# A hybrid decoder layer on one core: in the second feed-forward part, gate and up of ten chunks are computed as pairs with seven block products in two of four k steps

## The chip, the cores and the metric

The kernel runs on one core of one Trainium2 chip. The metric is the device time of one execution in microseconds. The engines are named as in the profile: PE (TensorE, matrix products), PEld (its weight loads), DVE (VectorE), ACT (ScalarE), POOL (GpSimd) and SP (SyncE, which issues most DMAs).

## What is computed

A decoder layer over 256 positions with a model width of 2048, in f32: a first SwiGLU feed-forward part (width 5632), a mixer (a state-space group beside a gated group, with a projection in and out), a second SwiGLU part, a gated per-layer embedding, and norms. The change is in the second feed-forward part:

```
def swiglu(x, w_gate, w_up, w_down):
    return (jax.nn.silu(x @ w_gate) * (x @ w_up)) @ w_down
h = h + 0.5 * swiglu(rms_norm(h, norm_ffn2[i]), w2_gate[i], w2_up[i], w2_down[i])
```

x is 256 by 2048, w_gate and w_up are 2048 by 5632, w_down is 5632 by 2048.

## The kernel before

**Products.** Every f32 product a·w is made of three matmuls of rounded parts: a high, w high; a high, w low; a low, w high. The activations (transposed, in hTh and hTl) are the stationary operand, 128 by 128; the weights stream as 512 columns. The weights come from DRAM as raw tiles of four k tiles by 512 columns (1 MB), and each half of a tile (two k tiles) is split: ACT copies it to `wh` in the rounded type (line 133), DVE subtracts to give `wl` (line 134). There are three raw buffers and four of each split (`LA_SPLIT` + 1).

**Order.** A program-wide list `plan` holds groups (one weight matrix, 512 columns) and their k steps. `stream` walks it in sub-steps of two k tiles: 12 matmuls for both blocks of 128 positions (t = 0, 1), into two accumulators. Before the products of sub-step i it emits the splits up to i + 3. A raw load is issued on SP two loads ahead; it waits for the last split that read its buffer. After a group's last sub-step its `post` is started; a post is a generator whose `yield n` puts its next piece n ticks later, and a tick is one sub-step. So a piece that is emitted after the products of sub-step i stands in the queues of DVE and ACT behind the split of i + 3 and ahead of that of i + 4. All engines work their queues in order.

**The feed-forward part** (`ffn_groups`, called for both). It takes 11 chunks of 512 columns. Per chunk there is a gate group (16 k tiles, 8 sub-steps) and an up group. `gate_post` puts silu of the scaled gate into g (ACT, line 393); `up_post` multiplies with up on DVE (line 404), and `flip` turns g: two 32x32 block transposes on DVE (line 367), a write to a DRAM scratch `gsc` (POOL queue, line 370) and four reads back (line 373). Six ticks later ACT and DVE split the turned g into gT (lines 203, 204). The down groups then run over 44 k tiles in the order of the chunks. gT is held in SBUF for all 11 chunks, in two tiles, gTa (six chunks) and gTb (five).

**PSUM.** Two pools of four banks: `acc` for the groups, `aux` for transposes and the mixer's small products. In the feed-forward part a chunk's gate and up take two `acc` banks each.

**Before the second part** the output projection of the mixer updates h (line 900), and `h_to_T` turns h into hTh and hTl: by `flip` and scaling for column blocks 0 and 2 in this place, by PE transposes for 1 and 3.

Of the kernel before, what the change touches and what calls it, by code (L numbers as in the profile page):

```python
# [15 lines left out]
P = 128  # L16
# [5 lines left out]
NW = 512  # L22
# [25 lines left out]

class Group:
    def __init__(self, w, n0, kt, act, post, kbase=0):  # L50
        self.w, self.n0, self.kt, self.act, self.post, self.kbase = w, n0, kt, act, post, kbase
        self.ps = None


class Layer:
# [38 lines left out]
    def stream(self):  # L94
        nc = self.nc
        subs, loads = [], []
        for g, k0, nk in self.plan:
            li = len(loads)
            loads.append((g, k0, nk))
# [3 lines left out]
        tail = self.plan[-1][0]  # L103
        n_tail = sum(sb[0] is tail for sb in subs)
        raws, split = {}, {}
# [10 lines left out]

        def do_split():
            i = state["sp"]
            state["sp"] += 1
            g, li, s0, k0, nk = subs[i]  # L120
            while state["ld"] <= min(li + 2, len(loads) - 1):
                load(state["ld"])
                state["ld"] += 1
            for f in self.presplit.pop(i, ()):
                f()
            src = raws[li][:, s0:s0 + nk, :]
# [11 lines left out]
        def products(i, ts, ps=None, c0=0, c1=NW):  # L138
            g, li, s0, k0, nk = subs[i]
            wh, wl = split[i]  # L140
            for j in range(nk):
                k = k0 + j
                for t in ts:
                    ah, al = g.act(k, t)
                    first, last = k == 0, k == g.kt - 1
                    o = (ps or g.ps[t])[:, c0:c1]
                    nc.tensor.matmul(o, ah, wh[:, j, c0:c1], start=first, stop=False)  # L147
                    nc.tensor.matmul(o, ah, wl[:, j, c0:c1], start=False, stop=False)  # L148
                    nc.tensor.matmul(o, al, wh[:, j, c0:c1], start=False, stop=last)  # L149

        for i in range(n):
            ahead = i + LA_SPLIT + 1
            if i > n - 2 * n_tail:
                ahead += (i - (n - 2 * n_tail)) // 2
            while state["sp"] < min(ahead, n):
                do_split()
            g, li, s0, k0, nk = subs[i]
            if k0 == 0:
                g.ps = [self.acc_p.tile([P, NW], F32, tag="acc", name=f"acc{t}") for t in range(2)]
            if g is tail:  # L160
                products(i, (0,))
            else:
                products(i, range(2))
                split.pop(i)
            if k0 + nk == g.kt:
                self.spawn(g.post(g, 0, 0) if g is tail else g.post(g))
            self.tick_no += 1
            self.run_due()
        late = self.acc_p.tile([P, NW], F32, tag="acc", name="late")
        for part, ps in enumerate((tail.ps[1], late)):  # L170
            for i in range(n - n_tail, n):
                products(i, (1,), ps, part * NW // 2, (part + 1) * NW // 2)
# [52 lines left out]
    def h_to_T(self, n, gcol, flip):  # L225

        if flip:
# [9 lines left out]
            for t in range(2):  # L237
                self.nc.vector.tensor_tensor(out=dl[:, t], in0=trv[:, t], in1=dh[:, t].bitcast(F32), op=ALU.subtract)
            return
        for b in range(2):  # L240
# [4 lines left out]
            self.split_gain2(ps, self.gcol[:, gcol + k0:gcol + k0 + 2], self.hTh[:, k0:k0 + 2], self.hTl[:, k0:k0 + 2])  # L245

# [3 lines left out]
    def kernel(self):  # L250
# [23 lines left out]
        self.gsc = [dram.tile([P, 4 * 256], F32, name=f"gsc{b}") for b in range(2)]  # L274
        self.spot = 0
# [13 lines left out]
        self.open("gta", "gt")  # L289
        self.open_g()  # L290
# [40 lines left out]
    def open(self, key, name, bufs=1):  # L331
        p = self.tc.tile_pool(name=name, bufs=bufs)
        self.pools[key] = p.__enter__()
        self.cms[key] = p
# [6 lines left out]
    KA = 24  # L341

    def open_g(self):
        n = self.KA // 4
        self.gT_a = (self.pools["gta"].tile([P, n, 4 * 256], F32R, name="gTah"),
                     self.pools["gta"].tile([P, n, 4 * 256], F32R, name="gTal"))
        self.open("gs", "gs")

    def open_gb(self):
        self.open("gtb", "gtb")  # L350
        n = 11 - self.KA // 4
        self.gT_b = (self.pools["gtb"].tile([P, n, 4 * 256], F32R, name="gTbh"),
                     self.pools["gtb"].tile([P, n, 4 * 256], F32R, name="gTbl"))

    def gT_at(self, c):
        if c < self.KA // 4:
            return self.gT_a, c
        return self.gT_b, c - self.KA // 4

    def flip(self, src):  # L360
# [9 lines left out]
        nc.gpsimd.dma_start(out=sc, in_=tr)  # L370
        sv = sc.rearrange("(i f) (a x) -> a f i x", i=4, a=4)
        for a in range(4):
            nc.gpsimd.dma_start(out=tr[32 * a:32 * a + 32, :].rearrange("f (i x) -> f i x", i=4), in_=sv[a])  # L373
        return tr

    def ffn_groups(self, which):
# [5 lines left out]
        def gate_post(c):  # L382
            def post(g):
                if which == 2 and c == 0:
                    self.close_mix()
                    self.open("gta", "gt")
                    self.open_g()
                    self.open_gb()
# [8 lines left out]
        def up_post(c):  # L397
            def post(g):
                gt = st.pop(c)
                if which == 1 and c == 6:  # L400
                    self.close("wrk")
                    self.open_gb()
# [3 lines left out]
                (th, tl), k = self.gT_at(c)  # L406
                tr = self.flip(gt)
                yield 6
                self.split_plain(tr.rearrange("p (i b u) -> p b i u", i=4, b=8),
                                 th[:, k, :].rearrange("p (b i u) -> p b i u", b=8, i=4),  # L410
                                 tl[:, k, :].rearrange("p (b i u) -> p b i u", b=8, i=4))
            return post

        def act_g(k, t):
            x, c = self.gT_at(k // 4)
# [17 lines left out]
        for c in range(11):  # L433
            gate = Group(wg, c * NW, 16, self.act_hT, gate_post(c))
            if which == 1 and c == 0:
                self.plan += [(gate, 0, 1), (gate, 1, 1)] + [(gate, k, 2) for k in (2, 4, 6)] + [(gate, 8, 4), (gate, 12, 4)]
            else:
                self.whole(gate)
            self.whole(Group(wu, c * NW, 16, self.act_hT, up_post(c)))
        for n in range(4):  # L440
            self.whole(Group(wd, n * NW, 44, act_g, down_post(n)))
# [216 lines left out]
    def close_mix(self):  # L658
        for n in ("yss", "mix", "qt"):
            self.close(n)  # L660

    def open_mix(self):
        for n in ("gtb", "gs", "gta"):
            self.close(n)
        self.open("qt", "qt", 2)
# [296 lines left out]
    def ple_groups(self):  # L962
# [4 lines left out]
        def prep():  # L967
            for n in ("gtb", "gs", "gta"):
# [161 lines left out]
```

## Time and profile before

| | before |
|---|---|
| median of 3 runs | 1851.09 us (1850.9 to 1851.18) |
| the profiled execution's own time | 1851.49 us |
| its span, first to last instruction | 1849.8 us |
| PE busy | 1837.9 us (99%), 8512 matmuls |
| DVE busy | 1140.3 us (62%), 1541 instructions |
| ACT busy | 854.5 us (46%) |
| POOL busy | 131.0 us (7%) |
| DMA | 405.10 MB, mean 219 GB/s |
| mean granted TensorE clock | 0.998 |

Times on the timeline are microseconds from the span's start. A PE that is busy is not a PE at its peak: matmuls are pipelined, so a recorded matmul lasts longer than the distance to the next one. The second feed-forward part begins at about 1022 us with the first gate, its down product at about 1501 us.

### The profile page before, as it was taken

To read this page: it belongs to the slowest core of one execution; us is meant where nothing else is said; L and a number is where in the kernel's file an instruction comes from. 1 tells how busy PE (TensorE), PEld (TensorE's weight loads), DVE (VectorE), ACT (ScalarE), POOL (GpSimd) and SP (SyncE) were. 2 spreads that over 40 slices of the span, in tenths; PEclk is the share of its full clock that TensorE was granted. 3 is DMA by queue.
4 is the path that set the end of the run, shared out by engine and by line. 5 is a ranking of instruction groups with operands and counts; after the bars stand their busy time and mean duration, and the time that the engine had idled before them with its cause. 6 is when DMAs were issued, how large, how long until landed. Compare 5 with 4: busy or idle time off the path is not lost.

```text
span 1849.8 us, 21900 instructions
## 1 busy us (share of the span) xinstructions
PE 1837.9 (99%) x8512; PEld 1526.8 (83%) x8512; DVE 1140.3 (62%) x1541; ACT 854.5 (46%) x1012; POOL 131.0 (7%) x208
## 2 busy tenths in 40 slices
PE   9999999999999999999999999999999999999998
PEld 7888888888888888888888888888888888888887
DVE  6788886555545554698876555555555555455565
ACT  6444444444444444444446544444444444444454
POOL 1000000000000000022100000000000000000000
PEclk9999999999999999999999999999999999999999
DMA  8677777666656665665546666666666665566553
GB/s 324 223 244 265 235 269 253 217 217 226 220 201 216 216 216 193 225 253 210 188 163 216 213 216 217 217 226 219 222 218 217 216 216 206 204 216 216 190 204 134
DMA packets 72615, 405.10 MB, mean 219 GB/s; under 512 B 10176, under 2 KB 15552, under 8 KB 29888
## 3 DMA queue, kind: packets, MB, share of 16 engines
q1 hardware_dynamic: 62000, 371.67, 56.4%
q0 software_dynamic: 10080, 31.47, 5.8%
q8 instruction: 66, 1.08, 0.2%
q10 hardware_dynamic: 432, 0.57, 0.1%
q14 instruction: 37, 0.30, 0.0%
HBM read 376.28 MB, written 27.26 MB: 218 GB/s over the span
## 4 chain that ended last, share of the span: by engine, by line
PE 98%; DMA 1%; issue 1%; DVE 0%; ACT 0%; SPq 0%; POOLq 0%; POOL 0%; DVEq 0%; ACTq 0%
PE acc L147 32%; PE acc L149 32%; PE acc L148 32%; PE tr L199 1%; PE y L759 1%; DMA raw<-in_w_gate 1%; PE v L712 0%; PE sp L800 0%; PE mps L623 0%; PE y L753 0%; DVE wl L134 0%; ACT wh L133 0%; SPq L296 0%; DVE hg L1052 0%; DVE h L1035 0%
## 5 line engine op out<-in xcount | busy, mean ns | idle before, releaser
L134 DVE TENSOR_TENSOR wl<-raw,wh 128x1024 fp32r<-128x1024 f32 (+1 forms) x649 | 800.9, 1237 | 642.5 <-ACT wh L133 640.7
L133 ACT ACTIVATE wh<-raw 128x1024 fp32r<-128x1024 f32 (+1 forms) x649 | 685.9, 1059 | 824.3 <-PE acc L149 779.6
L147 PE MATMUL acc<-wh,hTh 128*128 128x512 f32 (+1 forms) x1744 | 680.9, 390 | 0.1
L148 PE MATMUL acc<-wl,hTh 128*128 128x512 f32 (+1 forms) x1744 | 678.1, 389 | 1.3 <-DVE wl L134 1.3
L149 PE MATMUL acc<-wh,hTl 128*128 128x512 f32 (+1 forms) x1744 | 678.2, 389 | 0.0
L148 PEld LDWEIGHTS acc<-wl,hTh 128*128 128x128 f32 x1744 | 327.5, 188 | 69.1 <-DVE wl L134 2.1
L149 PEld LDWEIGHTS acc<-wh,hTl 128*128 128x128 f32 x1744 | 327.4, 188 | 68.2
L147 PEld LDWEIGHTS acc<-wh,hTh 128*128 128x128 f32 x1744 | 327.4, 188 | 67.8 <-ACT wh L133 0.5
L147 PE MATMUL acc<-wh,gTah 128*128 128x512 f32 x384 | 149.4, 389 | 0.0
L148 PE MATMUL acc<-wl,gTah 128*128 128x512 f32 x384 | 149.4, 389 | 0.0
L149 PE MATMUL acc<-wh,gTal 128*128 128x512 f32 x384 | 149.4, 389 | 0.0
L147 PE MATMUL acc<-wh,gTbh 128*128 128x512 f32 x320 | 124.5, 389 | 0.0
L148 PE MATMUL acc<-wl,gTbh 128*128 128x512 f32 x320 | 124.5, 389 | 0.0
L149 PE MATMUL acc<-wh,gTbl 128*128 128x512 f32 x320 | 124.5, 389 | 0.0
L370 POOL DMA_DIRECT2D gsc<-tr x30 | 17.0, 568 | 1160.1 <-DVE tr L367 1160.1
L147 PEld LDWEIGHTS acc<-wh,gTah 128*128 128x128 f32 x384 | 72.1, 188 | 15.1
L148 PEld LDWEIGHTS acc<-wl,gTah 128*128 128x128 f32 x384 | 72.1, 188 | 15.0
L149 PEld LDWEIGHTS acc<-wh,gTal 128*128 128x128 f32 x384 | 72.1, 188 | 14.9
L373 POOL DMA_DIRECT2D tr<-gsc x120 | 65.5, 552 | 97.4 <-DMA gsc<-tr 91.2
L147 PEld LDWEIGHTS acc<-wh,gTbh 128*128 128x128 f32 x320 | 60.1, 188 | 12.6
L148 PEld LDWEIGHTS acc<-wl,gTbh 128*128 128x128 f32 x320 | 60.1, 188 | 12.5
L149 PEld LDWEIGHTS acc<-wh,gTbl 128*128 128x128 f32 x320 | 60.1, 188 | 12.4
(233 smaller groups left out, 1061.5 us busy)
## 6 DMA issues: line engine op xcount, KB each, us to landing
raw<-in_w_up SPq DMA_DIRECT2D x88, 1024.0 KB, 5.8
raw<-in_w_down SPq DMA_DIRECT2D x88, 1024.0 KB, 4.8
raw<-in_w_gate SPq DMA_DIRECT2D x86, 1024.0 KB, 4.8
raw<-in_w_in SPq DMA_DIRECT2D x24, 1024.0 KB, 4.8
raw<-in_w_out SPq DMA_DIRECT2D x16, 1024.0 KB, 4.8
raw<-in_w_ple_gate SPq DMA_DIRECT2D x16, 1024.0 KB, 4.9
gsc<-tr POOLq DMA_DIRECT2D x30, 512.0 KB, 3.2
tr<-gsc POOLq DMA_DIRECT2D x120, 128.0 KB, 4.4
```

Source lines behind the costliest of these rows:

```text
L133: nc.scalar.activation(out=wh[:, 0:nk, :], in_=src, func=AF.Copy)
L134: nc.vector.tensor_tensor(out=wl[:, 0:nk, :], in0=src, in1=wh[:, 0:nk, :].bitcast(F32), op=ALU.subtract)
L147: nc.tensor.matmul(o, ah, wh[:, j, c0:c1], start=first, stop=False)
L148: nc.tensor.matmul(o, ah, wl[:, j, c0:c1], start=False, stop=False)
L149: nc.tensor.matmul(o, al, wh[:, j, c0:c1], start=False, stop=last)
L199: self.nc.tensor.transpose(ps[:, i * P:(i + 1) * P], b, self.ident)
L370: nc.gpsimd.dma_start(out=sc, in_=tr)
L373: nc.gpsimd.dma_start(out=tr[32 * a:32 * a + 32, :].rearrange("f (i x) -> f i x", i=4), in_=sv[a])
L759: nc.tensor.matmul(ps[:, 64 * i:64 * i + 64], R[ri][:, i, :], qt[:, f0:f0 + 64], start=False, stop=(a == 1 and ri == 1))
```

## The change

For chunks 1 to 10 of the second part, gate and up are one pair with the k steps S, N, S, N of four k tiles each (`steps_of`). An N step is as before: four k tiles of gate, then of up. An S step takes the two position blocks and the two halves of its four k tiles as a 2x2 block matrix A, the two k halves and gate and up as a 2x2 block matrix W, and makes the four blocks of A·W by Strassen's scheme (in Winograd's form) from seven block products of two k tiles, each in one PSUM bank: 42 matmuls where four times twelve were. P1, Q5, P6 and P7 take the four `aux` banks over both S steps; P2, Q4 and P3 add straight into the accumulators C0, C1 and C2, which the N steps use too.

The weight operands are g0, s1 = g0 + u0, g1, s2 = s1 + u1, s4 = s2 + g1, s3 = u0 + u1 and u1 (0 and 1 are the k halves); the four sums are made on DVE in f32 (`factor`), and each of the seven operands is split like a raw half. The sums of activation blocks are made once, after `h_to_T` of column blocks 0 and 2 (`sums_of_h`), and kept in S. An S step takes two loads, and from its fourth product on a third load ahead is issued.

After the second S step `aux_post` combines the four auxiliary banks (one copy on ACT, four adds on DVE); `gate_end` adds them to the gate accumulators and applies silu; `up_end` does the same for up, and two ticks later multiplies and turns g. In an S step three ticks pass over the seven products.

S, the sums' buffers and g's work tiles take SBUF, and gT of chunks 0 to 3 of the second part isn't kept there: `flip` writes the turned g to a DRAM tile `gsk` of its own and reads nothing back. When chunk 10 is done, the freed space becomes gTa (four chunks), and the four are read back into `land` and `tr` and split, between sub-steps of the first down group. The down groups run over the chunks 4 to 10, then 0 to 3. Pools are opened and closed in other places accordingly. The first feed-forward part keeps its order.

The core of the diff (blank lines left out):

```diff
+def steps_of(which, c):
+    return "SNSN" if which == 2 and c > 0 else None
...
+    ORDER = ("P1", "Q5", "P2", "P6", "Q4", "P7", "P3")
+    BANK = {"P2": "C0", "Q4": "C1", "P3": "C2"}
...
+            if e[0] == "S":
+                _, pair, k0 = e
+                loads += [(g, k0, KL) for g in pair.groups]
+                subs += [(pair, li, m, k0, 2) for m in range(7)]
+                continue
...
+        def add(li, name, x, y):
+            t = self.pools["sums"].tile([P, KS, NW], F32, tag="sum", name=name)
+            nc.vector.tensor_tensor(out=t, in0=x, in1=y, op=ALU.add)
+            sums[li, name] = t
+        def factor(li, m):
+            g0, g1, u0, u1 = (raws[li + x][:, y:y + 2, :] for x in range(2) for y in (0, 2))
+            if m == 0:
+                add(li, "s1", g0, u0)
+            if m == 1:
+                add(li, "s2", sums[li, "s1"], u1)
+            if m == 2:
+                add(li, "s4", sums[li, "s2"], g1)
+            if m == 3:
+                add(li, "s3", u0, u1)
+            return (g0, sums.get((li, "s1")), g1, sums.get((li, "s2")), sums.get((li, "s4")),
+                    sums.get((li, "s3")), u1)[m]
         def do_split():
             i = state["sp"]
             state["sp"] += 1
             g, li, s0, k0, nk = subs[i]
-            while state["ld"] <= min(li + 2, len(loads) - 1):
+            ahead = li + (3 if isinstance(g, Pair) and s0 > 2 else 2)
+            while state["ld"] <= min(ahead, len(loads) - 1):
                 load(state["ld"])
                 state["ld"] += 1
...
+            src = factor(li, s0) if isinstance(g, Pair) else raws[li][:, s0:s0 + nk, :]
...
+        def three(o, a, wh, wl, first, last):
+            nc.tensor.matmul(o, a[0], wh, start=first, stop=False)
+            nc.tensor.matmul(o, a[0], wl, start=False, stop=False)
+            nc.tensor.matmul(o, a[1], wh, start=False, stop=last)
+        def into(bank, a, wh, wl):
+            first = bank.left == bank.n
+            bank.left -= 3
+            three(bank.t, a, wh, wl, first, bank.left == 0)
+        def products(i, ts):
+            g, li, s0, k0, nk = subs[i]
+            wh, wl = split[i]
+            for j in range(nk):
+                for t in ts:
+                    into(g.banks[t], g.act(k0 + j, t), wh[:, j], wl[:, j])
...
+            if isinstance(g, Pair):
+                wh, wl = split.pop(i)
+                name = g.ORDER[s0]
+                for j in range(2):
+                    into(g.bank(name), self.act_S(name, k0, j), wh[:, j], wl[:, j])
+                if s0 == 6 and "S" not in g.steps[k0 // KL + 1:]:
+                    self.spawn(g.post())
+                self.tick_no += s0 % 2
+                self.run_due()
+                continue
...
+    def act_S(self, name, k0, j):
+        if name in ("P1", "P2", "Q4"):
+            return self.act_hT(k0 + j + 2 * (name != "P1"), int(name == "Q4"))
+        c = k0 // 8 * 1024 + ("Q5", "P6", "P7", "P3").index(name) * 256 + j * P
+        return tuple(x[:, c:c + P] for x in self.S)
+    def sums_of_h(self, n, tr):
+        nc = self.nc
+        if n == 0:
+            self.S = [self.pools["qt"].tile([P, BW], F32R, tag="qt", name=f"S{x}") for x in "hl"]
+        st = self.pools["yss"].tile([P, 1024], F32, tag="st", name="st")
+        a = tr.rearrange("p (i t kk u) -> p t kk i u", i=4, t=2, kk=4)
+        a11, a12, a21, a22 = (a[:, t, k:k + 2] for t in range(2) for k in (0, 2))
+        s1, s2, s3, s4 = (st[:, 256 * m:256 * m + 256].rearrange("p (kk i u) -> p kk i u", kk=2, i=4) for m in range(4))
+        for o, x, y, op in ((s1, a21, a22, ALU.subtract), (s2, s1, a11, ALU.subtract), (s3, a11, a21, ALU.subtract),
+                            (s4, a12, s2, ALU.add)):
+            nc.vector.tensor_tensor(out=o, in0=x, in1=y, op=op)
+        sh, sl = (x[:, 512 * n:512 * n + 1024] for x in self.S)
+        yield 1
+        self.split_plain(st, sh, sl)
...
+        if keep is not None:
+            nc.gpsimd.dma_start(out=self.gsk[keep], in_=tr)
+            return
...
+    def fetch(self, sc, tr):
         sv = sc.rearrange("(i f) (a x) -> a f i x", i=4, a=4)
         for a in range(4):
-            nc.gpsimd.dma_start(out=tr[32 * a:32 * a + 32, :].rearrange("f (i x) -> f i x", i=4), in_=sv[a])
-        return tr
+            self.nc.gpsimd.dma_start(out=tr[32 * a:32 * a + 32, :].rearrange("f (i x) -> f i x", i=4), in_=sv[a])
...
+        def turn(c, gt):
+            if which == 2 and c < self.KA[1]:
+                self.flip(gt, c)
+                return
+            tr = self.flip(gt)
+            if which == 1 or c < 10:
                 yield 6
-                self.split_plain(tr.rearrange("p (i b u) -> p b i u", i=4, b=8),
-                                 th[:, k, :].rearrange("p (b i u) -> p b i u", b=8, i=4),
-                                 tl[:, k, :].rearrange("p (b i u) -> p b i u", b=8, i=4))
-            return post
+                split_g(c, tr)
+                return
+            for x in ("sums", "gs", "qt"):
+                self.close(x)
+            self.open_g(2)
+            self.open("land", "land")
+            land = self.pools["land"].tile([P, 4 * 256], F32, name="land")
+            self.fetch(self.gsk[0], land)
+            yield 6
+            split_g(c, tr)
+            split_g(0, land)
+            self.fetch(self.gsk[1], tr)
+            self.fetch(self.gsk[2], land)
+            yield 5
+            split_g(1, tr)
+            self.fetch(self.gsk[3], tr)
+            yield 1
+            split_g(2, land)
+            yield 4
+            split_g(3, tr)
+        def pair_of(c, gate, up):
+            m = {}
+            def aux_post():
+                yield 1
+                pool, v = self.pools["gs"], self.nc.vector
+                p1, q5, p6, p7 = (pair.banks[x].t for x in ("P1", "Q5", "P6", "P7"))
+                a, b, y, z = (pool.tile([P, NW], F32, tag=x, name=x) for x in ("g0", "g1", "y", "z"))
+                self.nc.scalar.activation(out=a, in_=p1, func=AF.Copy)
+                v.tensor_tensor(out=b, in0=p6, in1=a, op=ALU.add)
+                v.tensor_tensor(out=y, in0=q5, in1=b, op=ALU.subtract)
+                v.tensor_tensor(out=b, in0=p7, in1=b, op=ALU.add)
+                v.tensor_tensor(out=z, in0=p7, in1=y, op=ALU.subtract)
+                m.update(g=(a, b), u=(y, z))
+            def gate_end(g):
+                yield 1
+                for t in range(2):
+                    x = m["g"][t]
+                    self.nc.vector.tensor_tensor(out=x, in0=g.ps[t], in1=x, op=ALU.add)
+                    self.nc.scalar.activation(out=x, in_=x, func=AF.Silu, scale=r[:, t:t + 1])
+            def up_end(g):
+                yield 1
+                for t, op in enumerate((ALU.add, ALU.subtract)):
+                    x = m["u"][t]
+                    self.nc.vector.tensor_tensor(out=x, in0=g.ps[t], in1=x, op=op)
+                yield 2
+                for t in range(2):
+                    x = m["g"][t]
+                    self.nc.vector.scalar_tensor_tensor(out=x, in0=m["u"][t], scalar=r[:, t:t + 1], in1=x,
+                                                        op0=ALU.mult, op1=ALU.mult)
+                yield from turn(c, m["g"])
+            gate.post, up.post = gate_end, up_end
+            pair = Pair(self, gate, up, steps_of(which, c), aux_post)
+            for j, x in enumerate(pair.steps):
+                self.plan += [("S", pair, 4 * j)] if x == "S" else [(gate, 4 * j, 4), (up, 4 * j, 4)]
...
+        first = 0 if which == 1 else self.KA[1]
         for n in range(4):
-            self.whole(Group(wd, n * NW, 44, act_g, down_post(n)))
+            g = Group(wd, n * NW, 44, act_g, down_post(n))
+            self.plan += [(g, 4 * (c % 11), 4) for c in range(first, first + 11)]
...
```

## Rows read from the trace of the kernel before

**Rows 1.** The page: each engine's busy time, and the chain that ended last.

```profile
PE 1837.9 (99%) x8512; PEld 1526.8 (83%) x8512; DVE 1140.3 (62%) x1541; ACT 854.5 (46%) x1012; POOL 131.0 (7%) x208
...
PE 98%; DMA 1%; issue 1%; DVE 0%; ACT 0%; SPq 0%; POOLq 0%; POOL 0%; DVEq 0%; ACTq 0%
```

**Rows 2.** A chunk: us, PE, PEld, DVE, ACT, POOL busy (count), PEclk, DMA, GB/s.

```profile
1109.60:1153.20 43.60, 43.60 (x194) 36.12 (x193) 23.33 (x22) 19.30 (x19) 2.74 (x5) 1.00 0.64 217
```

**Rows 3.** DVE timeline of one chunk: start, us, operation, idle before.

```profile
1109.69 1.40 DVE L404 SCALAR_TENSOR_TENSOR g<-acc,r,g 128x512 f32<-128x512 f32 x2
1111.01 1.29 DVE L367 STREAM_TRANSPOSE tr<-g 128x512 f32<-128x512 f32 x2
1112.22 1.18 DVE L134 TENSOR_TENSOR wl<-raw,wh 128x1024 fp32r<-128x1024 f32 x1
...
1116.70 1.23 DVE L134 TENSOR_TENSOR wl<-raw,wh 128x1024 fp32r<-128x1024 f32 x1 [1.49 <-ACT wh L133]
...
1153.21 1.40 DVE L404 SCALAR_TENSOR_TENSOR g<-acc,r,g 128x512 f32<-128x512 f32 x2
```

**Rows 4.** DVE groups over the span: count, busy us, mean ns, idle before.

```profile
L134 DVE TENSOR_TENSOR wl<-raw,wh 128x1024 fp32r<-128x1024 f32 x647 | 799.5, 1238 | 639.9 <-ACT wh L133 638.1
...
L423 DVE SCALAR_TENSOR_TENSOR h<-acc,h 128x512 f32<-128x512 f32 x16 | 10.3, 682 | 0.0
...
L717 DVE TENSOR_TENSOR te<-v,qt 128x256 f32<-128x256 f32 x16 | 6.7, 416 | 0.0
```

**Rows 5.** DVE timeline where it is queued without idle time.

```profile
72.16 1.22 DVE L204 TENSOR_TENSOR gTal<-tr,gTah 128x1024 fp32r<-128x1024 f32 x1 [1.38 <-ACT gTah L203]
73.30 1.22 DVE L134 TENSOR_TENSOR wl<-raw,wh 128x1024 fp32r<-128x1024 f32 x1
74.43 0.29 DVE L511 TENSOR_SCALAR A<-A 128x256 f32<-128x256 f32 x1
...
81.09 0.18 DVE L523 TENSOR_TENSOR t<-prm 128x32 f32<-128x32 f32 x1
81.31 0.19 DVE L527 TENSOR_TENSOR den<-t,t 128x32 f32<-128x32 f32 x1
```

**Rows 6.** ACT timeline: two silus of a chunk, the split after.

```profile
1131.25 1.37 ACT L393 ACTIVATE g<-acc,r 128x512 f32<-128x512 f32 x2 [0.98 <-PE acc L149]
1132.52 1.05 ACT L133 ACTIVATE wh<-raw 128x1024 fp32r<-128x1024 f32 x1
```

**Rows 7.** SP's waits in ten chunks: us in total, times, longest.

```profile
SPq L114 <- DVE wl L134: 402.6, 80, 6.6
```

**Rows 8.** Timelines of SP and POOL: DMA issues around one flip.

```profile
1107.08 0.33 SPq L114 DMA_DIRECT2D raw<-in_w_gate  x1
...
1112.59 0.56 POOL L370 DMA_DIRECT2D gsc<-tr  x1 [37.16 <-DVE tr L367]
...
1113.43 4.85 SPq L114 DMA_DIRECT2D raw<-in_w_up  x2
...
1116.36 2.18 POOL L373 DMA_DIRECT2D tr<-gsc  x4 [3.20 <-DMA gsc<-tr]
```

**Rows 9.** DMA issues at 1107.1, 1113.4, 1112.6, 1118.0: KB, us to landing.

```profile
raw<-in_w_gate SPq DMA_DIRECT2D x1, 1024.0 KB, 4.8
...
raw<-in_w_up SPq DMA_DIRECT2D x1, 1024.0 KB, 6.0
gsc<-tr POOLq DMA_DIRECT2D x1, 512.0 KB, 3.2
...
raw<-in_w_up SPq DMA_DIRECT2D x1, 1024.0 KB, 8.4
```

**Rows 10.** A stretch near the start, columns as in Rows 2.

```profile
20.00:25.00 5.00, 4.18 (x18) 3.26 (x18) 4.97 (x7) 4.88 (x10) 0.00 (x0) 1.00 1.03 434
```

**Rows 11.** A stretch at the mixer's end, columns as in Rows 2.

```profile
1030.00:1040.00 10.00, 10.00 (x46) 8.28 (x45) 6.94 (x8) 6.03 (x9) 0.00 (x0) 1.00 0.57 206
```

**Rows 12.** DVE timeline in the down product: chunk 10's split.

```profile
1518.15 1.23 DVE L204 TENSOR_TENSOR gTbl<-tr,gTbh 128x1024 fp32r<-128x1024 f32 x1 [0.38 <-ACT gTbh L203]
```

More of the change, by code (lines that the diff above doesn't have):

```diff
@@ L51, in __init__, with bank @@
         self.w, self.n0, self.kt, self.act, self.post, self.kbase = w, n0, kt, act, post, kbase
-        self.ps = None
+        self.ps, self.left, self.pair = None, kt, None
+class Pair:
+    ORDER = ("P1", "Q5", "P2", "P6", "Q4", "P7", "P3")
+    BANK = {"P2": "C0", "Q4": "C1", "P3": "C2"}
+    def __init__(self, layer, gate, up, steps, post):
+        self.layer, self.groups, self.steps, self.post = layer, (gate, up), steps, post
+        gate.pair = up.pair = self
+        self.banks = {}
+    def bank(self, name):
+        name = self.BANK.get(name, name)
+        if name not in self.banks:
+            L = self.layer
+            n = 6 * self.steps.count("S") * (name != "C3")
+            if name[0] == "C":
+                n += 12 * self.steps.count("N")
+                t = L.acc_p.tile([P, NW], F32, tag="acc", name=name)
+            else:
+                t = L.aux_p.tile([P, NW], F32, tag="aux", name=name)
+            self.banks[name] = Bank(t, n)
+        return self.banks[name]
 class Layer:
@@ L102, in stream @@
         n = len(subs)
-        tail = self.plan[-1][0]
+        tail = subs[-1][0]
         n_tail = sum(sb[0] is tail for sb in subs)
-        raws, split = {}, {}
+        raws, split, sums = {}, {}, {}
         state = {"ld": 0, "sp": 0}
@@ L142, in products @@
                 k = k0 + j
[L143 to L149, printed above, removed]
+                three(ps[:, c0:c1], g.act(k, t), wh[:, j, c0:c1], wl[:, j, c0:c1], k == 0, k == g.kt - 1)
         for i in range(n):
@@ L157, in stream @@
             g, li, s0, k0, nk = subs[i]
-            if k0 == 0:
-                g.ps = [self.acc_p.tile([P, NW], F32, tag="acc", name=f"acc{t}") for t in range(2)]
+            if isinstance(g, Pair):
[8 more added lines that the diff above has]
+                continue
+            if g.ps is None:
+                if g is tail:
+                    g.ps = [self.acc_p.tile([P, NW], F32, tag="acc", name=f"acc{t}") for t in range(2)]
+                else:
+                    if g.pair:
+                        x = 2 * g.pair.groups.index(g)
+                        g.banks = [g.pair.bank(f"C{x + t}") for t in range(2)]
+                    else:
+                        g.banks = [Bank(self.acc_p.tile([P, NW], F32, tag="acc", name=f"acc{t}"), 3 * g.kt)
+                                   for t in range(2)]
+                    g.ps = [b.t for b in g.banks]
             if g is tail:
-                products(i, (0,))
+                tail_products(i, 0, g.ps[0])
+                done = k0 + nk == g.kt
             else:
@@ L164, in stream @@
                 split.pop(i)
-            if k0 + nk == g.kt:
+                done = g.banks[0].left == 0
+            if done:
                 self.spawn(g.post(g, 0, 0) if g is tail else g.post(g))
@@ L171, in stream @@
             for i in range(n - n_tail, n):
-                products(i, (1,), ps, part * NW // 2, (part + 1) * NW // 2)
+                tail_products(i, 1, ps, part * NW // 2, (part + 1) * NW // 2)
                 self.tick_no += 1
@@ L274 @@
         self.gsc = [dram.tile([P, 4 * 256], F32, name=f"gsc{b}") for b in range(2)]
+        self.gsk = [dram.tile([P, 4 * 256], F32, name=f"gsk{c}") for c in range(self.KA[1])]
         self.spot = 0
@@ L967, in prep @@
         def prep():
-            for n in ("gtb", "gs", "gta"):
+            for n in ("land", "gta", "gtb"):
                 self.close(n)
```

81 lines of the change are left out of this document (48 added, 33 removed).

## The prediction, made before the changed kernel ran

> **What bounds the kernel now.** I read the busy shares and the chain of waits first: TensorE (PE) is busy 99% of the span and is 98% of the chain, VectorE (DVE) 62% [rows 1]. Averages over all stages don't decide a change in one, so the stretches of the second FFN come next: in a gate/up chunk of 43.6 us PE is busy throughout, DVE 23.3 us, ScalarE (ACT) 19.3 us [rows 2]. In DVE's own order the scaling of one chunk's product with g starts at 1109.69 and that of the next at 1153.21: a chunk takes 43.52 us [rows 3]. It has 2 x 16 x 2 x 3 = 192 matmuls of 512 columns, so one takes 226.7 ns, and a sub-step (two k tiles, 12 matmuls) 2.72 us. The stage is bound by PE, and DVE rests 1.5 us before nearly every split [rows 3].
>
> **What goes from PE.** In chunks 1 to 10, two of four k steps become seven block products of two k tiles and three matmuls, 42 instead of 48. That is 6 x 2 x 10 = 120 matmuls less, 27.2 us, if PE stays the bound. A chunk is then 180 matmuls, 40.8 us.
>
> **What comes to DVE.** An S step has 4 weight sums and 7 splits (wl), where the same loads had 4 splits before; an N step keeps 4. Per chunk that is 2 x 11 + 2 x 4 = 30 operations of 128x1024, where there were 16. Alone one lasts 1.23 to 1.24 us [rows 4], but queued back to back the next independent one starts 1.13 to 1.14 us after it (72.16 to 73.30 to 74.43); an operation that reads the result just ahead of it starts about 0.1 us later (81.09 to 81.31 for one that lasts 0.18) [rows 5]. The sums are placed one operation ahead of their readers, so I take 1.135 us: 34.05 us. An add of f32 512 columns from PSUM isn't in the trace; its nearest row is the h update from PSUM without a pointer scalar, 682 ns [rows 4], and with the same 0.08 us of overlap it takes 0.605 us. Bounds are 0.57 (half of 1.135) and 0.66 (the start spacing of the g scaling, 1109.69 to 1111.01 for two), which is 0.3 to 0.4 a chunk either way. Eight of them, with 0.1 for the dependent one: 4.94. The two scalings are 1.32 and the two transposes 1.21 [rows 3]. Sum: 41.5 us a chunk, and 1.14 more where an earlier chunk's g is split: chunks 5 to 10, since chunks 0 to 3 are kept away and 4 to 9 are split one chunk later. So **DVE needs 41.5 to 42.65 us where PE needs 40.8.** DVE becomes the bound of the stage, at almost the old time, before any wait of its own.
>
> **What DVE waits for.** With DVE as the bound each idle time on it counts.
> - (1) ACT in its silu. The gate end adds t=0 and t=1 on DVE just before S's sum s4, and ACT's two silus stand ahead of its copy wh of the third product. ACT starts 0.7 us after the first add starts, takes 1.27 for two silus (1131.25 to 1132.52) and 1.06 for wh [rows 6], so wl can start at 0.7 + 1.27 + 1.09 = 3.1; DVE is done with both adds and s4 at 1.21 + 1.14 = 2.35. Idle 0.74 a chunk.
> - (2) The load of the up weights of an S step. There are three raw buffers, and this load goes into the one of the N step's gate, free only after that gate's second wl: now too SP waits for a wl before each load [rows 7]. Behind that wl DVE has two splits of up (2.27) and then s1, which needs the load. In one N step of a chunk the auxiliary adds (2.52) stand in between, in the other the scalings and transposes (2.53): 4.8 us of work. An undisturbed load is issued 0.03 us after the wl ends (that end is 0.09 after DVE is free), takes 0.33 to issue [rows 8] and 4.8 to land [rows 9]: 5.25. I count the landing from the end of the issue, since the write issued at 1112.59 in 0.56 lands after 3.2 and its reads start at 1116.36 [rows 8]. Idle 0.45. But the load of S's gate is issued only 2.3 us earlier, into the same engines. They moved 434 GB/s when full [rows 10], so 1 MB is at least 2.4 us, and two such loads 2.3 apart cost the second about 0.2. Idle 0.65 in the N step with the auxiliary adds.
> - (3) In the other N step the write of the transposed g is issued by POOL about 2.8 us after the load. In the trace the load that is issued at 1113.43, 0.84 after such a write, lands after 6.0 instead of 4.8, and the next, beside the four reads, after 8.4 [rows 8, 9]. The reads come later than this load; of the 1.2 that the write costs I take half. Idle 1.25, between 0 (the queued work covers all) and 4.05 (a load beside the reads: 8.4 + 0.45 - 4.8).
>
> Sum of (1) to (3): 2.6 us a chunk; low 0.74, high 0.74 + 1.65 + 4.05 = 6.4, with 6.0 for the load in (2).
>
> PE can't hide this: it may run only four split buffers behind DVE, and with DVE slower over each whole chunk that lead is used up in the first one. For chunk 1 I take 42.0, as DVE enters it with its lead. Behind DVE's late wl nobody but PE waits; SP's loads wait for the same wl, which is (2).
>
> **The sum.** 42.0 + 3 x (41.5 + 2.6) + 6 x (42.65 + 2.6) = 445.8 against 10 x 43.52 = 435.2: +10.6 us. The profiled execution took 1851.49 us (span 1849.8), 0.4 above the median 1851.09: 1851.1 + 10.6 = **1862 us**.
>
> **Costed at nothing.** The sums of h at the end of the mixer: 8 adds of 128x256 (0.42 each as a product of that size [rows 4]) and 2 splits, 5.6 us of DVE and 2.1 of ACT, where DVE is busy 6.9 of 10 us [rows 11]; three sub-steps of splits lie ahead of PE. Without that cover, 5.6. The four kept chunks: POOL writes them once (0.56) and issues their 16 reads while the down product runs; the same splits (1.23 on DVE) then come beside wl, where DVE has 1.5 free in each 2.72, as chunk 10's split has now [rows 12]. The tightest is chunk 1: 4 + 4 reads issued on POOL (4.4) and about 7 to land, against 13.6 us of five sub-steps; if late, 1 to 3 us of PE. POOL's queue holds nothing else there. The banks: the next pair's C0 and P1 are read out by DVE before the wl that their products wait for. PE's gaps: near the start PE stood still for 0.82 of 5 us with the granted clock at 1.00 [rows 10]; here I expect about 0.9 before a product in part of a chunk.
>
> **A rule against the change.** The Trainium skill ("VectorE: DVE Perf Modes", Terms) says that every DVE operation is followed by a drain and the next can't issue until the pipeline is empty. The trace disagrees for independent operations: the next starts 0.08 to 0.09 before the recorded end of the one before [rows 5].
>
> **Rivals.**
> - *DVE's recorded spacing doesn't hold, each operation costs its full duration* (the rule above gives this): 30 x 1.235 + 8 x 0.685 + 1.48 + 1.37 = 45.4 and 1.23, with 2.6 idle: 42 + 3 x 48.0 + 6 x 49.2 = 481, 1897 us. Against it: rows 5. 3%.
> - *The loads collide in full*: idle 6.4, 42 + 3 x 47.9 + 6 x 49.05 = 480, 1896; half way there 1879. For it: 6.0 and 8.4 were seen [rows 9]. Against: the reads come 3 us after this load's issue. 12% for 1876 and above.
> - *Faster: the queued DVE work hides the loads.* If a load lands in under 4.8 us of its wl and only (1) is left, the period is 42.2 and 43.4: 42 + 126.6 + 260.4 = 429, 1845 us. It decides at the landing time: each 0.5 us on both loads of a chunk is 9 us of the total. For it: the transfer alone could be nearly in time. Against: 4.8 is also what undisturbed loads took. 13%.
> - *PE stays the bound* (DVE doesn't matter): 1824 us. Against: the count. 2%.
>
> **How the numbers follow.** The forecast has 70%, its own range 1851 to 1875 (idle 1.5 to 4 a chunk). The range that should hold 8 in 10 takes in the faster case's edge: 1845 to 1878. About 0.2%, 3.7 us, is what a measurement of this kernel tells from no change. Faster by more than that (below 1847.4): 0.15, the faster rivals; within it (to 1854.8): 0.13, the low end of the forecast, idle of about 1 to 1.6; slower: 0.72.
>
> **What would show it.** In the changed kernel's chunks 2 to 10: DVE busy nearly without gaps, a period of 44 to 45.5 us; PE's waits released by wl, mostly in the first S step of a chunk; DVE's own waits at s1, released by the load of up weights, about 0.7 and 1.25 us, and one at the third wl, released by ACT. The down products and the mixer keep their times. It is wrong if PE's rows run without waits (then DVE's operations are shorter or fewer than I count), or if DVE's spacing isn't 1.13 to 1.14, or if the loss sits in the first sub-steps of the down product.

## The result, and the profile of the changed kernel

The changed kernel takes 1861.55 us (median of 4 runs, 1860.59 to 1864.34) against 1851.13 for the kernel before beside it: ratio 1.0061 [1.0049, 1.0073], 10.4 us slower. The profiled execution took 1861.93 us with a span of 1860.1 and a mean granted clock of 0.998, as before.

The page of the changed kernel, busy times and the chain that ended last:

```profile
PE 1827.5 (98%) x8392; PEld 1500.8 (81%) x8392; DVE 1342.2 (72%) x1771; ACT 918.1 (49%) x1084; POOL 129.7 (7%) x208
...
PE 75%; DVE 15%; DMA 6%; issue 2%; ACT 1%; POOL 0%; SPq 0%; DVEq 0%; POOLq 0%; ACTq 0%
```

Against [rows 1], 120 matmuls are gone as the change says, and DVE has 202 us more. The chain shows what that did: 15% of it is now DVE and 6% DMA, where PE had 98%. The share of busy time alone (PE still 98%) would have hidden it.

Two stretches of the same kernel, each from one chunk's transposes to the next's (columns as in [rows 2]): chunk 2's to chunk 3's, and chunk 4's, the first whose g is split beside the pairs, to chunk 5's.

```profile
1167.17:1213.30 46.13, 42.83 (x182) 33.34 (x181) 41.86 (x43) 24.50 (x25) 0.53 (x1) 1.00 0.52 195
1257.90:1303.14 45.24, 42.86 (x182) 33.36 (x181) 42.92 (x44) 25.36 (x26) 2.75 (x5) 1.00 0.57 209
```

DVE's 23.3 us of [rows 2] have become 41.9 and 42.9, more than the 40.8 that PE needs.

DVE's timeline in the second of these stretches, to be laid beside [rows 3] (start, us, operation, idle before it in brackets):

```profile
1257.90 1.30 DVE L487 STREAM_TRANSPOSE tr<-g 128x512 f32<-128x512 f32 x2
1259.12 2.32 DVE L197 TENSOR_TENSOR wl<-raw,wh 128x1024 fp32r<-128x1024 f32 x2
1263.06 1.23 DVE L162 TENSOR_TENSOR s<-raw 128x1024 f32<-128x1024 f32 x1 [1.62 <-DMA raw<-in_w_up]
1264.20 1.22 DVE L197 TENSOR_TENSOR wl<-raw,wh 128x1024 fp32r<-128x1024 f32 x1
1265.34 1.22 DVE L162 TENSOR_TENSOR s<-s,raw 128x1024 f32<-128x1024 f32 x1
...
1276.69 4.63 DVE L197 TENSOR_TENSOR wl<-raw,wh 128x1024 fp32r<-128x1024 f32 x4
1281.23 0.68 DVE L579 TENSOR_TENSOR g<-P,g 128x512 f32<-128x512 f32 x1
1281.95 0.69 DVE L580 TENSOR_TENSOR y<-Q,g 128x512 f32<-128x512 f32 x1
1282.68 0.69 DVE L581 TENSOR_TENSOR g<-P,g 128x512 f32<-128x512 f32 x1
1283.29 0.68 DVE L582 TENSOR_TENSOR z<-P,y 128x512 f32<-128x512 f32 x1
1283.94 1.23 DVE L162 TENSOR_TENSOR s<-raw 128x1024 f32<-128x1024 f32 x1
...
1288.49 1.28 DVE L589 TENSOR_TENSOR g<-C,g 128x512 f32<-128x512 f32 x2
1289.69 1.22 DVE L162 TENSOR_TENSOR s<-s,raw 128x1024 f32<-128x1024 f32 x1
1291.53 1.22 DVE L197 TENSOR_TENSOR wl<-raw,wh 128x1024 fp32r<-128x1024 f32 x1 [0.63 <-ACT wh L196]
```

The 1.5 us of rest before each split are gone. The stretch holds the second S step of chunk 5 and then the first of chunk 6. What is left are two kinds of wait: s1 for the up weights (L162, 1.62 us here, at the other s1 none) and the third wl of a chunk's first S step for ACT (0.63). DVE's groups from 1066 to 1513 us (count, busy us, mean ns, idle before) have their sums over the stage; of the 7.7 us for ACT, 1.8 are a wait at 1512.71, which already belongs to the down product:

```profile
L197 DVE TENSOR_TENSOR wl<-raw,wh 128x1024 fp32r<-128x1024 f32 x142 | 167.6, 1217 | 7.8 <-ACT wh L196 7.7
L197 DVE TENSOR_TENSOR wl<-s,wh 128x1024 fp32r<-128x1024 f32 x79 | 93.7, 1218 | 0.0
L162 DVE TENSOR_TENSOR s<-raw 128x1024 f32<-128x1024 f32 x39 | 47.6, 1221 | 18.5 <-DMA raw<-in_w_up 18.3
```

PE's weight loads now wait for DVE (engine, line, waited for: us in total, times, longest, same stretch):

```profile
PEld P L203 <- DVE wl L197: 24.0, 27, 1.1
PEld C L203 <- DVE wl L197: 13.1, 20, 1.1
```

The distance from PE's first matmul of chunk 1 to its first of the down product is 1067.02 to 1512.29, 445.3 us, where it was 1066.45 to 1501.65, 435.2. So 10.1 of the 10.4 us lie in the ten chunks.

### The profile page after: what moved, and what is told of

It is laid out like the page before. It is cut to its first block, busy times and chain, and to the rows that moved or that the text cites. A ratio compares the mean times of both kernels' runs of the same rounds, so it can differ in the third digit from the quotient of the medians.

```text
span 1860.1 us, 22003 instructions
## 1 busy us (share of the span) xinstructions
PE 1827.5 (98%) x8392; PEld 1500.8 (81%) x8392; DVE 1342.2 (72%) x1771; ACT 918.1 (49%) x1084; POOL 129.7 (7%) x208
## 4 chain that ended last, share of the span: by engine, by line
PE 75%; DVE 15%; DMA 6%; issue 2%; ACT 1%; POOL 0%; SPq 0%; DVEq 0%; POOLq 0%; ACTq 0%
PE acc L202 23%; PE acc L203 23%; PE acc L204 23%; DVE wl L197 9%; DMA raw<-in_w_up 4%; DVE s L162 4%; PE C L203 1%; PE C L202 1%; PE C L204 1%; DMA tr<-gsc 1%; ACT wh L196 1%; PE y L959 1%; DMA raw<-in_w_gate 1%; PE tr L294 1%; PE v L912 0%
## 5 line engine op out<-in xcount | busy, mean ns | idle before, releaser
L202 PE MATMUL acc<-wh,hTh 128*128 128x512 f32 (+1 forms) x1104 | 432.0, 391 | 0.1
L203 PE MATMUL acc<-wl,hTh 128*128 128x512 f32 (+1 forms) x1104 | 429.3, 389 | 1.6 <-DVE wl L197 1.6
L204 PE MATMUL acc<-wh,hTl 128*128 128x512 f32 (+1 forms) x1104 | 429.3, 389 | 0.0
L203 PEld LDWEIGHTS acc<-wl,hTh 128*128 128x128 f32 x1104 | 207.4, 188 | 45.0 <-DVE wl L197 3.0
L202 PEld LDWEIGHTS acc<-wh,hTh 128*128 128x128 f32 x1104 | 207.3, 188 | 43.1 <-ACT wh L196 0.5
L204 PEld LDWEIGHTS acc<-wh,hTl 128*128 128x128 f32 x1104 | 207.3, 188 | 42.9
L203 PE MATMUL C<-wl,hTh 128*128 128x512 f32 x400 | 157.7, 394 | 6.5 <-DVE wl L197 6.3
L202 PE MATMUL C<-wh,hTh 128*128 128x512 f32 x400 | 156.8, 392 | 1.2 <-ACT wh L196 1.2
L204 PE MATMUL C<-wh,hTl 128*128 128x512 f32 x400 | 156.1, 390 | 0.0
L197 DVE TENSOR_TENSOR wl<-s,wh 128x1024 fp32r<-128x1024 f32 x80 | 94.9, 1218 | 0.4 <-ACT wh L196 0.4
```

Of the source, the lines that this page charges most:

```text
L197: nc.vector.tensor_tensor(out=wl[:, 0:nk, :], in0=src, in1=wh[:, 0:nk, :].bitcast(F32), op=ALU.subtract)
L202: nc.tensor.matmul(o, a[0], wh, start=first, stop=False)
L203: nc.tensor.matmul(o, a[0], wl, start=False, stop=False)
L204: nc.tensor.matmul(o, a[1], wh, start=False, stop=last)
```

## The experiments

Each is the changed kernel with the edit shown, timed beside the kernel before; ratios are against that.

**The form alone.** Everything else stays (pools, sums of h, kept chunks, order of the down product), but every k step is an N step.

```diff
-    return "SNSN" if which == 2 and c > 0 else None
+    return None
```

> The changed kernel with no S step: gate and up as before the change, but chunks 0 to 3 of g still kept in DRAM, the sums of h still made, the pools and the order of the down product as changed. Theory (DVE bounds the S steps): the loss goes, about 1851.7 us (before plus the 0.6 us that PE waits at the start of the second part). Rival (the kept chunks, the moved pools and the read-back cost the time): it stays near the changed kernel's 1861.6.

1851.74 us, 1.0004 [0.9994, 1.0013]. The sums of h, the kept chunks, their 16 reads in the down product and the moved pools together cost nothing that can be told from no change; the loss belongs to the S steps.

**Is PE the bound?** One matmul of three is left out in every S step: 14 of 42, 280 in all, of the 1800 that the ten chunks have.

```diff
+        def two(bank, a, wh, wl):
...
+            nc.tensor.matmul(bank.t, a[0], wh, start=first, stop=False)
+            nc.tensor.matmul(bank.t, a[0], wl, start=False, stop=last)
...
-                    into(g.bank(name), self.act_S(name, k0, j), wh[:, j], wl[:, j])
+                    two(g.bank(name), self.act_S(name, k0, j), wh[:, j], wl[:, j])
```

> Each S product without its third matmul (activations' low part times weights' high part is left out): 28 matmuls of 227 ns less per chunk, 280 in all, 63 us of PE. Theory: DVE sets the pace, so nearly nothing is gained: 1855 to 1862 us. Rival (PE's work and waits that come on top of it, such as banks or the start of matmuls after a wait, set the pace): 1861.6 - 63 = about 1798.

1858.98 us, 1.0045 [1.0030, 1.0060]. 280 matmuls less are 63.5 us of PE at 226.7 ns; the kernel gained 2.6. Two stretches of it, one chunk long each (columns as in [rows 2]):

```profile
1213.00:1258.00 45.00, 40.37 (x157) 30.53 (x157) 42.76 (x44) 24.98 (x26) 0.80 (x2) 0.92 0.55 206
1258.00:1303.00 45.00, 40.82 (x154) 30.95 (x153) 42.37 (x43) 24.84 (x26) 2.78 (x5) 0.89 0.57 207
```

DVE's 42.8 and 42.4 of 45 us are what they were, and set the pace. The granted clock isn't 1.00 here (last section), but that doesn't eat up the saving: at 0.89 the 152 matmuls that a chunk has left (34.5 us at 226.7 ns) are an estimated 38.7 us, some 6 less than a chunk took.

**One DVE operation less in each S step.** The sum s3 isn't made.

```diff
-            if m == 3:
-                add(li, "s3", u0, u1)
...
-                    sums.get((li, "s3")), u1)[m]
+                    u0, u1)[m]
```

> Without the weight sum s3 (the operand is u0 instead, so that product is another): one DVE operation of 1.135 us less per S step, 2.27 a chunk, everything else as it is. Theory: each chunk from 2 on gets shorter by about 2.27 us, 1841 us (1839 to 1845). Rival (the landing of the S loads sets the pace and DVE only waits for it): DVE's wait before s1 grows by what is saved, 1857 to 1861.

1841.43 us, 0.9951 [0.9937, 0.9966]: 20.1 us for 20 operations, 1.0 us each. Taking away 5% of DVE's work in the stage (22.7 us at 1.135) turns the loss into a gain; taking away 16% of PE's did almost nothing.

**The wait for ACT.** Both silus a tick later, behind the copy that wl needs.

```diff
+                yield 1
+                for t in range(2):
+                    x = m["g"][t]
```

> The two silus of a pair's gate end one tick after the adds that feed them, so that ACT's copy wh of the third product no longer stands behind them. Theory: DVE's wait of 0.63 us for that wh goes, once a chunk in chunks 2 to 10, and counts in full, as the loads are issued behind DVE's own splits: 1861.6 - 5.7 = 1856 us (1854 to 1858). Rival (DVE's idle time is made up for elsewhere, by the wait for the load): 1860 to 1862.

1853.86 us, 1.0015 [1.0006, 1.0025], 7.7 us less than the changed kernel; I had expected 5.7. DVE's waits for ACT from 1110 to 1500, nine with 5.6 us in all, are gone. That is most of the gain. The other 2 us aren't traced to one cause: DVE's waits for the load are 17.0 us in the stage, where they were 18.3, and each kernel's runs spread over 4 to 5 us.

**The wait for the load.** In S steps the up load brings half its tile.

```diff
+            if g.pair and g.pair.steps[k0 // KL] == "S" and g is g.pair.groups[1]:
+                nk = KS
...
+            u0 = u1 = raws[li + 1][:, 0:2, :]
```

> The up load of each S step brings only its first half (512 KB), and u0 stands for u1 (so the S products are others); operations and their order are as in the changed kernel. Theory: this load is the one that DVE waits for before s1, 16.6 us in all; half the transfer is over about 1.2 us sooner and disturbs its neighbour less, so 8 to 13 us of the waits go: 1849 to 1854 us. Rival (this wait is not on the path): 1860 to 1862.

1849.03 us, 0.9990 [0.9981, 0.9999], 12.5 us less. DVE's waits from 1110 to 1500 us, first the changed kernel, then this one:

```profile
DVE s L162 <- DMA raw<-in_w_up: 12.9, 13, 2.8
DVE wl L197 <- ACT wh L196: 5.6, 9, 0.6
```

```profile
DVE wl L200 <- ACT wh L199: 8.1, 14, 1.8
DVE s L164 <- DMA raw<-in_w_up: 1.9, 3, 0.8
```

11.0 us of waiting for the load went, and with them most of the 12.5. (The wait of 1.8 for ACT belongs to the down product, which begins at 1497.45 in this run.)

**s3 on POOL**, which is busy 7% of the span.

```diff
-            nc.vector.tensor_tensor(out=t, in0=x, in1=y, op=ALU.add)
+            (nc.gpsimd if name == "s3" else nc.vector).tensor_tensor(out=t, in0=x, in1=y, op=ALU.add)
```

> The weight sum s3 is made on POOL instead of DVE, two operations of 128x1024 a chunk. Theory: DVE has 2.27 us a chunk less, so 1841 us as without s3, if POOL's operation disturbs nobody. Rival: DVE and POOL get in each other's way, as wl took 1.67 to 1.9 us instead of 1.23 beside POOL's products in the mixer; a POOL operation of 128x512 lasted 1.3 to 2.1 us there, so one of 1024 some 2.6 to 4.3, and what DVE loses beside it eats half or all of the gain: 1850 to 1866.

1874.19 us, 1.0122 [1.0107, 1.0137], 12.6 slower than the changed kernel and outside both expectations. POOL's and DVE's timelines around one s3:

```profile
1204.96 2.40 POOL L162 TENSOR_TENSOR s<-raw 128x1024 f32<-128x1024 f32 x1 [19.11 <-DVE wl L197]
```

```profile
1204.74 1.28 DVE L589 TENSOR_TENSOR g<-C,g 128x512 f32<-128x512 f32 x2
1205.94 2.50 DVE L162 TENSOR_TENSOR s<-s,raw 128x1024 f32<-128x1024 f32 x1
1208.37 1.21 DVE L197 TENSOR_TENSOR wl<-raw,wh 128x1024 fp32r<-128x1024 f32 x1
```

While POOL adds, DVE's adds with an operand in PSUM take their usual 1.28 for two; the next one, with two operands in SBUF, ends only 1.08 us after POOL's, twice as long as its 1.22. This is the first S step of a chunk. In the second, POOL's add begins beside a sum that already runs on DVE (1227.74 to 1228.96) and is 0.86 us longer, and the wl behind that sum is held up:

```profile
1227.97 3.26 POOL L162 TENSOR_TENSOR s<-raw 128x1024 f32<-128x1024 f32 x1 [6.97 <-DVE wl L197]
```

```profile
1228.88 3.43 DVE L197 TENSOR_TENSOR wl<-raw,wh 128x1024 fp32r<-128x1024 f32 x1
```

Here too DVE's operation ends 1.08 us after POOL's. A chunk loses 1.28 + 2.21 = 3.5 us in this way where it saves 2.27; over ten chunks that is 12.2, about the 12.6 measured. DVE is busy 1357.8 us in this kernel, 15.6 more with 20 operations fewer. The Trainium skill ("SBUF — State Buffer", section "SBUF: two separate sides") says that a DVE operation with two SBUF inputs and a POOL operation that reads SBUF exclude one another, and that the later one stands until the first has ended. The trace agrees, with 2.50 and 3.43 us against 1.22.

**One S step instead of two**, first of the four. By the count below DVE then needs 34.8 us a chunk and PE 42.2.

```diff
-    return "SNSN" if which == 2 and c > 0 else None
+    return "SNNN" if which == 2 and c > 0 else None
```

> One S step per chunk instead of two (S, N, N, N). DVE then has 23 long operations a chunk, 26.1 us, plus 8.7 of the small ones and the split of g: 34.8 us against PE's 186 matmuls, 42.2 us. Theory: PE bounds every chunk, 60 matmuls are saved against before, 13.6 us: 1838 us (1837 to 1840). Rival (a pair costs something of its own whatever DVE's load, by its banks, posts and loads): half of the gain or less, 1845 to 1851.

1846.95 us (9 runs, 1845.1 to 1849.93), 0.9980 [0.9970, 0.9989]: a gain, but 9 us short of 1838. With less work ahead of it on DVE the split of g, six ticks after the transposes, comes to its turn 14.2 us after them (chunk 4's, 1249.23 to 1263.47), where it was 17.7 in the changed kernel (1257.90 to 1275.56), and its reads, issued from 1256.93 on, haven't landed. The reads take longer too: 7.5 us to landing (median of the four), beside loads issued at 1257.71 and 1260.78, where in the changed kernel they took 3.2 and no load was issued while they ran (1264.84 to 1269.5). ACT's timeline, then DVE's:

```profile
1267.15 1.06 ACT L298 ACTIVATE gTbh<-tr 128x1024 fp32r<-128x1024 f32 x1 [4.93 <-DMA tr<-gsc]
```

```profile
1268.24 1.22 DVE L299 TENSOR_TENSOR gTbl<-tr,gTbh 128x1024 fp32r<-128x1024 f32 x1 [4.77 <-ACT gTbh L298]
...
1275.57 1.23 DVE L162 TENSOR_TENSOR s<-raw 128x1024 f32<-128x1024 f32 x1 [2.69 <-DMA raw<-in_w_up]
```

Everything behind that split waits 4.8 us with it; SP's next loads wait for splits behind it, and s1 for such a load. Five such waits come to 15.9 us of DVE's idle time. Two of them reach PE: chunks 6 and 8 take 45.5 and 45.0 us, the others 42.4 to 42.8. I had left this wait out of the 1838.

**The same, with the split of g ten ticks after the transposes.**

```diff
-                yield 6
+                yield 6 if which == 1 else 10
```

> One S step per chunk, and the split of the turned g ten ticks after the transposes instead of six. In the run with one S step ACT stood up to 4.8 us before that split for the reads of g from DRAM, from chunk 5 on, and the weight splits behind it came late. Theory: without that wait PE bounds all chunks: 1838 us (1837 to 1840). Rival (a pair costs PE something of its own): 1844 to 1847 as without the delay.

1845.36 us, 0.9969 [0.9957, 0.9981]: again short. The wait for the reads is gone, and PE's chunks take 42.4 to 42.8 up to the fifth; from the sixth on they take 43.0 to 43.7. DVE's timeline shows why: at ten ticks the split stands among the sums of the only S step, where DVE has no rest, and PE's weight loads wait there (7.9 us in 15 waits in the whole stage). The first five chunks have no such split in their S step, as chunks 0 to 3 are kept away.

```profile
1358.10 1.23 DVE L162 TENSOR_TENSOR s<-raw 128x1024 f32<-128x1024 f32 x1 [0.25 <-DMA raw<-in_w_up]
1359.35 1.23 DVE L197 TENSOR_TENSOR wl<-raw,wh 128x1024 fp32r<-128x1024 f32 x1
1360.49 1.22 DVE L299 TENSOR_TENSOR gTbl<-tr,gTbh 128x1024 fp32r<-128x1024 f32 x1
1361.63 1.22 DVE L162 TENSOR_TENSOR s<-s,raw 128x1024 f32<-128x1024 f32 x1
```

**The S step third of the four, the split of g late.** On DVE the S step then comes behind the transposes and ahead of the split of g.

```diff
-    return "SNSN" if which == 2 and c > 0 else None
+    return "NNSN" if which == 2 and c > 0 else None
...
-                yield 6
+                yield 6 if which == 1 else 10
```

> One S step per chunk, in the third place (N, N, S, N), and the split of the turned g ten ticks after the transposes. With the S step first, the gate's and up's last adds of the chunk before, the silus and the split of g fall into the S step, where DVE already has its eleven long operations, and PE waited up to 0.6 us per chunk from chunk 6 on. Theory: away from them DVE keeps its lead, and every chunk takes what the best ones took there, 42.45 us: 1841 us (1840 to 1843; 10.6 saved in the ten chunks, 0.6 lost at their start). Rival (a pair's S step costs PE the same wherever it stands): 1844 to 1846.

1840.20 us (1840.11 to 1840.25), 0.9941 [0.9926, 0.9956], 10.7 us faster than the kernel before. A chunk is 42.4 us, PE busy throughout, and DVE's only waits are for ACT, as in the kernel before, and cost nothing. A chunk's window and DVE's waits (1066 to 1490 us):

```profile
1236.90:1279.30 42.40, 42.40 (x188) 34.94 (x187) 35.63 (x37) 22.57 (x24) 2.75 (x5) 1.00 0.60 220
```

```profile
DVE wl L197 <- ACT wh L196: 63.4, 110, 1.8
```

**That, with the silus a tick later.** The edits are those of this experiment and of the one on ACT's wait together.

> As the one before, with the two silus of the gate one tick after their adds. Theory: in this place no S product stands behind the silus, so it changes nothing: 1841 us, within 1 us of the one before. Rival (ACT's order still holds up a split): 1 to 4 us faster than it.

1839.98 us, 0.9939 [0.9923, 0.9956]: no difference, as expected where DVE is no longer the bound. What was worth 7.7 us in the changed kernel is worth nothing here.

## Why the prediction was right

**The bound.** "DVE becomes the bound of the stage, at almost the old time, before any wait of its own" held: 120 matmuls left PE, and the chain moved to DVE. The run with 280 matmuls fewer and the one with 20 sums fewer show it from both sides. The rival in which PE stays the bound fell with them.

**DVE's work.** Forecast 41.5 and 42.65 us a chunk, measured 41.9 and 42.9. The long operations start 1.13 to 1.14 us apart, as in [rows 5]: four splits from 1276.69 to 1281.23. The adds from PSUM, whose price I had from a neighbour, start 0.60 apart where they are independent (two from 1288.49 to 1289.69). The forecast had 0.605. The four auxiliary adds take 2.71, not 2.52: the second reads the result just ahead of it, the third overwrites what the second reads, and both start 0.72 to 0.73 after the one ahead; I had counted 0.1 for one. The rest, some 0.1 to 0.2, is that the operation ahead of a wait counts in full, with 1.22 and not 1.135.

The rule that the prediction weighed (the Trainium skill, "VectorE: DVE Perf Modes", Terms: no next operation before the drain is over) doesn't show in a stage that DVE bounds either: independent operations start 0.08 before the recorded end of the one before. Only dependent ones pay, some 0.1. The prediction took the rule without its exception: on the same page the Trainium skill (section "The DRAIN you can't avoid") lets a next operation that is not held start earlier, as the independent ones do here.

**DVE's waits** in chunks 2 to 10. (1) For ACT 0.63, forecast 0.74, once a chunk. (3) For the up load in the N step with the flip, nine waits of 0.40, 2.82, 1.82, 1.62, 0.49, 0.54, 1.33, 0.31 and 1.75: 1.23 on average, forecast 1.25. (2) In the N step with the auxiliary adds 1.61 (before chunk 2, at 1104.82), 0.13, 0.75, 0.22, 0.52, 0.36, 0.07 and twice nothing: 0.41 on average, forecast 0.65. This is the term that was mis-sized: the load lands 5.2 us after its issue on average, where I had 5.33 (0.33 + 4.8 + 0.2), and 4.9 us of work are queued behind the issue, where I had 4.8. The mechanism of (3) can be read off the issues of one such step, SP's and POOL's, with their landings (us from issue):

```profile
1163.69 0.33 SPq L157 DMA_DIRECT2D raw<-in_w_gate  x1
1165.96 0.33 SPq L157 DMA_DIRECT2D raw<-in_w_up  x1
```

```profile
1168.77 0.53 POOL L489 DMA_DIRECT2D gsk<-tr  x1 [42.60 <-DVE tr L487]
```

```profile
raw<-in_w_gate SPq DMA_DIRECT2D x1, 1024.0 KB, 6.5
raw<-in_w_up SPq DMA_DIRECT2D x1, 1024.0 KB, 7.5
gsk<-tr POOLq DMA_DIRECT2D x1, 512.0 KB, 6.0
```

The loads are 2.27 us apart (forecast 2.3), the write comes 2.8 after the second (forecast 2.8), and s1 waited 2.82 there: the landing less 4.7 us of queued work (forecast 4.8). The next two such loads land after 6.5 and 6.3 and cost 1.82 and 1.62, those that land after 5.1 and 5.0 cost 0.49 and 0.31: the landing less 4.7 each time. So the wait is the landing's length and nothing else, as forecast; why one load lands after 5.0 and the next after 7.5, no run here tells.

Behind both sizes stands a misreading. I counted the landing from the end of the issue, but the view counts it from its start: the up load issued at 1279.08 lands after 4.8, and s1, which reads it, starts at 1283.94. That put 0.33 too much into (2) and (3). Against it, what other transfers add to the 4.8 was sized too low, 0.2 in (2) and 0.8 in (3) where the landings show 0.4 and 1.1 on average. That (3) came out at 1.23 was luck.

**The sum.** Ten chunks took 445.3 us, forecast 445.8, but by two errors that nearly cancel. For chunks 2 to 10 I had 380.4 us of DVE work and 23.4 of idle; measured are 383.1 (3 x 41.86 + 6 x 42.92) and 20.3 (445.3 less chunk 1's 41.9 and the work), which the three kinds of wait add up to as well (5.6 + 3.7 + 11.1 = 20.4). Nor are they even: from first matmul to first matmul, chunks 2 to 4 took 45.1 each against 44.1 forecast, the other six 44.7 against 45.25. The size was right to about 3 us of work and 3 of waiting; that the total is closer was luck. The rivals of the loads (6.4 of idle a chunk, or loads hidden) are refuted by 2.3 of idle a chunk (20.3 / 9), the rival in which each operation costs its full duration by the spacing.

**Costed at nothing.** The kept chunks and the banks cost nothing: PE waits neither at the read-backs nor for a bank. The sums of h were to be covered, and were not quite. Those of block 0 (four adds and the split Sl, 1007.45 to 1008.92 and 1010.84 to 1011.97) stand on DVE ahead of the update of h for block 2. Its transposes start at 1014.43, where they started at 1012.44; the turned h is back later, ACT's scaling waits 3.32 for it, and PE once 0.6 for a split, which it didn't before. The 6.9 of 10 us in [rows 11] are read at 1030, behind the mixer, where the sums of block 2 come; where those of block 0 come, from 1005 to 1015, DVE was already busy 8.3 of 10 us before. There was room for the work, but not for what was queued behind it.

**What I got wrong later.** That one S step would give most of its 13.6 us (6 x 10 matmuls) came true only in the third run of it. Both misses were the split of g, which had cost nothing in the changed kernel and whose place I hadn't worked out anew: six ticks are no fixed time, nor is the landing of the reads.

## What to carry to other kernels

Before PE's work is traded for work on another engine, add up that engine's whole queue over a stage, at its start-to-start spacing: here each saved group of six matmuls (1.36 us) was bought with seven DVE operations (7.9 us), which is free only up to the rest that DVE has in a chunk. Two S steps used up more than the rest, one S step fits, and then its place decides: behind the transposes and ahead of the late split. (The third place with the split at six ticks wasn't run.) A delay that is counted in steps of another queue has to be worked out again when that queue's work changes.

## What the runs showed of the hardware that was not expected

In the run with two matmuls the granted clock fell in every chunk but the first of the ten. Its windows over one such place (columns as in [rows 2]):

```profile
1267.00:1268.50 1.50, 0.85 (x4) 0.67 (x4) 1.50 (x2) 0.63 (x1) 0.00 (x0) 1.00 0.09 30
1268.50:1270.00 1.50, 0.43 (x3) 0.09 (x1) 1.50 (x3) 1.16 (x2) 0.00 (x0) 1.00 0.74 191
1270.00:1271.50 1.50, 1.50 (x5) 1.17 (x6) 1.50 (x2) 1.50 (x2) 0.00 (x0) 0.65 1.02 431
1271.50:1273.00 1.50, 1.50 (x5) 1.17 (x4) 1.50 (x2) 1.50 (x3) 0.00 (x0) 0.50 0.20 82
1273.00:1274.50 1.50, 1.50 (x6) 1.18 (x5) 1.50 (x3) 1.10 (x2) 0.00 (x0) 0.71 0.34 44
1274.50:1276.00 1.50, 1.36 (x7) 0.78 (x6) 1.50 (x2) 1.50 (x2) 0.00 (x0) 1.00 0.65 262
```

PE stood still for over half of 3 us (1.28 busy), then had about 4 us in which the clock was partly or wholly at its lower level, 1.2 GHz, and came back to 2.4. What the lower clock alone cost there wasn't separated. In the changed kernel, whose weight loads wait for wl up to 1.1 us at a time and not 2.0 as here, the clock stays at 1.00 in every chunk. In the run with s3 on POOL, where they wait up to 3.2 us at a time, it was 0.96 from 1067 to 1113 and 0.97 from 1157 to 1206, but 1.00 in the stretches between and behind (1113 to 1157 and 1206 to 1250); what decides there isn't shown.

Most matmuls of an S step, and the first ones behind it, start 0.23 to 0.24 us apart even without a wait (1068.38, 1068.62, 1068.86 for Q's first three) where those of an N step have 0.227, and a chunk of the last two kernels takes 42.4 us where 186 matmuls at 226.7 ns are 42.2: about 0.2 us an S step, cause unknown.
